# Retention decode: query-times-state products in blocks of eight, and a value-spreading product of 128 rows

## The chip, the core and the metric

The kernel runs on one core of one Trainium2 chip. The metric is the time of one execution on the device, in microseconds (us). A core has TensorE for matrix products (PE in the profile, its weight loads PEld), VectorE (DVE), ScalarE (ACT), GpSimd (POOL) and SyncE (SP), and sixteen DMA engines that move data between HBM and the on-chip memory. The engines run side by side and wait for each other through semaphores; each engine takes its own instructions in the order in which they stand.

## What is computed

One inference step of a two-layer decoder for a new sequence of 256 tokens and for eight decode samples of one token each, 264 columns in all. Layer 0 mixes by RWKV-7, layer 1 by retention; before and after each mixer stands half a SwiGLU. The change touches layer 1's mixer. Its four heads have keys of 256 and values of 512. Cut to the samples, the reference computes for each head and each of the eight samples:

```
q = rotate(x @ wq); k = rotate((x @ wk) / 16); v = x @ wv
S = S * g_head + outer(k, v)          # state [256, 512], read from and written to HBM
o = q @ S                             # [512]
out = (silu(x @ wg) * head_norm(o)) @ wo
```

All is float32. The large products (x @ w) are made of three one-pass products of values split in a high and a low part; the small ones are plain float32 products, each of which stands in the trace as two records.

## The kernel before

**The stream.** All weights pass as 364 units of eight 128x128 tiles through `wt` (L184): SP loads a unit into one of three `raw` buffers, ACT rounds it into `hi` (L89), DVE takes the rest into `lo` (L104), three buffers each, and TensorE makes three products of 264 columns for each tile (`mm3`, L136).

**Who sets the order.** `weave` (L198) writes the program out: a main generator with the large products, and side generators whose steps are put between them when the kernel's own estimate of the engines' times says that they are ready; `mm` (L135) gives the estimate of a product. The framework then orders each engine's instructions once more at compile time by a model of its own. `keep_in_program_order` ties an instruction behind the one that was written before it on its engine, and nothing ties the products.

**Retention.** `retnet` (L1186) makes, head by head, q, k, v and a gate as the main stream (`stream`, L1213). Beside it, `attend` (L1289) makes a head's 256 new tokens, and `decode` (L1366) its eight samples. At the start of a head `attend` turns the samples' rows of v (partitions 0 to 7) into `vr`, a tile of 40 partitions: the high parts at partitions 0 to 7, the low parts at 32 to 39 and zeros between them, which ACT writes anew for each head. For a sample b, `decode` then spreads its row over all 128 partitions with one one-pass product (`pv = sel[:, b, :].T @ vr`, 40 rows, 512 columns), ACT scales the state S (128 x 2 x 512: two halves `kt` of the keys), DVE adds `k * v` to each half (L113), and POOL's queue sends the new state out (L1385). After each pair of samples come four products of q with the states, one for each half of the keys and each sample of the pair: 128 rows, 32 columns of the array, 512 columns of S. Each writes its own quarter of the partitions of one PSUM tile, so a set of four fills the array's four column groups, and the four pairs of a head add up there. `qm` holds the q columns with zeros around them.

**State buffers.** The 32 states pass through ten buffers (`NSB`), loaded by SP in the queue of the weights (`load`, L1168). Six are loaded ahead; the step of sample i asks for state i+6, which takes the buffer of sample i-4 and so waits until that one's products with q, and its transfer out, are done.

Of the kernel before, what the change touches and what calls it, by code (L numbers as in the profile page):

```python
# [40 lines left out]
class Step:  # L41
    def __init__(self, ctx, nc, tc, io):
# [9 lines left out]
        self.late = nc.gpsimd   # the queue of transfers that wait for results  # L52
# [13 lines left out]
    def use(self, m):  # L66
        """the estimates' factors on an engine's times, and the times from an engine to the next"""
        self.model = m
        self.factor = dict(pe=m["PEF"], dve=m["DVEF"], act=m["ACTF"], pool=1.0)
        self.lag = dict(pe=m["LP"], dve=m["LD"], act=m["LA"], pool=0.15)  # L70
# [16 lines left out]
    def act(self, out, in_, func=AF.Copy, scale=1.0, bias=None):  # L87
# [3 lines left out]
        if table != self.table:  # L91
            self.tc.keep_in_program_order(ins)   # no more changes of table than there are in this order
# [30 lines left out]
    def vec(self, name, in_, out, **kw):  # L123
        """another operation of the vector engine"""
        ins = getattr(self.nc.vector, name)(in_=in_, out=out, **kw)
        self.pin(ins)
        self.spent("dve", 0.07 + (0.0064 if name == "reciprocal" else 0.00104) * cols(in_), out, in_)

    def turn(self, out, in_):
        """32x32 blocks transposed"""  # L130
# [4 lines left out]
    def mm(self, out, lhsT, rhs, start=True, stop=True):  # L135
        self.nc.tensor.matmul(out=out, lhsT=lhsT, rhs=rhs, start=start, stop=stop)  # L136
        m, n = cols(lhsT), cols(rhs) / 2400
        if rhs.dtype == F32R:
            us = n + 0.003
        elif m > 64:  # L140
            us = max(4 * n, 0.215)
        else:
            us = max(4 * n * 0.66, 0.09) if m > 32 else 0.035
# [13 lines left out]
    def split(self, raw, first=False):  # L157
        hi = self.hi_p.tile([128, UT, 128], F32R, tag="hi", name="hi")
        lo = self.lo_p.tile([128, UT, 128], F32R, tag="lo", name="lo")
        now, start, self.start = self.now, self.start, 0.0   # it runs ahead  # L160
# [11 lines left out]
    def wt(self, key, k, m, whole=False):  # L172
        """A tile in its two parts, or as it is for a float32 product."""
# [12 lines left out]
    def beside(self, rank, *gs):  # L186
        """more steps for between, those of a lower rank first"""
# [10 lines left out]
    def weave(self, main, sides=()):  # L198
        """Issues main's steps and, between them, the steps of self.sides. A step that yields a key goes on when that
        key is marked; else when its instructions should be through, and the yielded microseconds over."""  # L200
# [56 lines left out]
    def feed(self, f, gain, tail=None):  # L257
        """x[f] has its new value: its square sum, and its parts times the gain; the tail's columns stand behind them."""
# [34 lines left out]
    def setup(self):  # L293
# [8 lines left out]
        # the first weights and inputs, in the order of their use; meanwhile products of nothing keep TensorE's clock up  # L302
# [14 lines left out]
    def preload(self, func):  # L317
        """the table of a function that comes soon"""
        self.act(self.one, self.eps6, func)

# [66 lines left out]
def pack_x(a):  # L387
    """[tokens, 1024] -> [128, 8, tokens]"""
# [35 lines left out]
class Rwkv(Step):  # L424
    def rw_consts(self, p):
        """[128, n] columns by name."""
# [11 lines left out]
    def rwkv(self, gain):  # L438
# [6 lines left out]
        with ExitStack() as ctx:  # L445
# [22 lines left out]
            # 0.5 w0, 0.5 a0, 0.5 ka, 1 - 0.5 ka  # L468
# [9 lines left out]
            # T's tiles: zeros that no product writes  # L478
# [3 lines left out]
            # per pair of heads: [., halves, chunk, 64] operands of the chunks' transitions, with their identities  # L482
# [11 lines left out]
            # lora inputs by linearity: xs @ W = h @ W + (prev - h) @ (mu W)  # L494
# [13 lines left out]
            # of the eight samples, feature-major: log d, kk, -kk a, k', r, v  # L508
# [3 lines left out]
            sto = P1.tile([128, KT, 64], F32, name="sto")   # final states, [key, value]  # L512
# [9 lines left out]
            def stream():  # L522
# [3 lines left out]
                for k0, k1 in ((0, TU["RK"]), (TU["RK"], KT)):  # L526
# [5 lines left out]
                    if rs is None:  # L532
                        rs = self.rms()
                        # normalised inputs, their differences to the step before, and the mixes
# [52 lines left out]
                # the sum, at first without the last heads  # L587
# [90 lines left out]
            # k = xk @ wk, four output tiles at a time, and the lengths of k * k_k per head  # L678
# [26 lines left out]
            # decays and rates of a pair of heads  # L705
# [31 lines left out]
            # alpha, beta, kappa  # L737
            def stage(f):
# [12 lines left out]
                # k' = k (1 - ka + ka a), a = (1 + ta) / 2  # L751
# [15 lines left out]
                # A = alpha beta', token-major: what is below the diagonal, by 32x32 blocks  # L767
# [12 lines left out]
            # T = (I - A)^-1 = I + T A: the 32x32 blocks on its diagonal by substitution, a block on two partitions, one for  # L780
            # the even and one for the odd rows; the rest of each 64x64 by products
            both = lambda t: (t[:, 0:512], t[:, 512:1024])

            def inverse(g):
# [17 lines left out]
                # X[c, i] = T[i, c]  # L802
# [42 lines left out]
            # v token-major, on the other half's partitions  # L845
# [26 lines left out]
            # the state after a chunk and its rows are products of the state before and the chunk's values with one matrix  # L872
            # [keys and earlier steps, (keys, steps)]: first that matrix, then the recurrence
# [4 lines left out]
            def head(f):  # L878
# [12 lines left out]
                # earlier steps' beta' with rho and alone  # L891
# [7 lines left out]
                # alpha kappa' and alpha  # L899
# [8 lines left out]
                # T times both  # L908
# [23 lines left out]
                for c in range(NC):  # L932
                    if c == 2:
                        yield f"L{f}1"
                        # the bonus of a step for itself
# [13 lines left out]
                # group norm per head, token-major  # L949
# [18 lines left out]
                # y = (norm * g + b + bonus) * gate  # L968
# [18 lines left out]
            # one step for the eight samples: 128 rows (half, pair, sample), [value, key] states  # L987
# [8 lines left out]
            def states_with(row, out):  # L996
                """the old states' products with a key each"""
# [26 lines left out]
            def decode_rows():  # L1024
                """S' r = S (d r) + (S kk) (b r) + v (k' r)"""
# [42 lines left out]
    def new_states(self, pool):  # L1068
        """S' = S d + (S kk) b' + v k'"""
# [43 lines left out]
def eye():  # L1113
    """[(j h n), (i c)]: a block's even or odd rows of the identity"""
# [4 lines left out]
def consts():  # L1119
    """Constants of the shapes alone."""  # L1120
# [29 lines left out]
def pack_wkv(s):  # L1150
    """[b, (f e), v, k] -> [(e f b), (v k)]"""
# [10 lines left out]
class Ret(Rwkv):  # L1162
# [21 lines left out]
    def retnet(self, gain):  # L1184
        nc, tc, ps_ = self.nc, self.tc, self.ps
        xg = self.xg  # L1186
        with ExitStack() as ctx:
# [9 lines left out]
            sel = P1.tile([40, NS, 128], F32R, name="sel")  # L1197
            s40 = P1.tile([40, NS], F32, name="s40")
            self.tt(s40, ident[0:40, 0:NS], ident[0:40, 32:32 + NS], ALU.add)
            self.act(sel, s40.unsqueeze(2).to_broadcast([40, NS, 128]))  # L1200
# [12 lines left out]
            def stream():  # L1213
# [36 lines left out]
                # the sum, at first without the last head  # L1250
# [38 lines left out]
            def attend(h, q, k, v):  # L1289
                yield f"v{h}"  # L1290
                # v's sample rows in two parts at partitions 0 and 32
# [3 lines left out]
                vr = P.tile([40, DV], F32R, tag="vr", name="vr", bufs=2)  # L1295
                self.act(vr, c[0:40, RC["dmat"]:RC["dmat"] + DV], scale=0.0)
# [3 lines left out]
                # token-major v  # L1300
# [232 lines left out]
```

## Time and profile before

| | us |
|---|---|
| three runs | 1349.78, 1350.78, 1352.82 |
| median of the runs | 1350.78 |
| the profiled execution: its span from first to last instruction | 1357.0 |
| in it: retention beside the stream | about 870 to 1098 |
| TensorE busy, share of the span | 97% |
| VectorE busy | 66% |
| ScalarE busy | 51% |

The profile is one execution of the program. Of it the trace has the span alone, and nothing of what lies around it; the span stands 6.2 us above the median of the runs. A matrix product's record begins when it starts and ends at a modelled time, and products overlap; so starts are compared with starts below. A row of the timeline with "x2" or more merges records of one kind that follow each other.

### The profile page before, as it was taken

To read this page: it belongs to the slowest core of one execution; us is meant where nothing else is said; L and a number is where in the kernel's file an instruction comes from. 1 tells how busy PE (TensorE), PEld (TensorE's weight loads), DVE (VectorE), ACT (ScalarE), POOL (GpSimd) and SP (SyncE) were. 2 spreads that over 40 slices of the span, in tenths; PEclk is the share of its full clock that TensorE was granted. 3 is DMA by queue.
4 is the path that set the end of the run, shared out by engine and by line. 5 is a ranking of instruction groups with operands and counts; after the bars stand their busy time and mean duration, and the time that the engine had idled before them with its cause. 6 is when DMAs were issued, how large, how long until landed. Compare 5 with 4: busy or idle time off the path is not lost.

```text
span 1357.0 us, 26335 instructions
## 1 busy us (share of the span) xinstructions
PE 1320.5 (97%) x10620; PEld 1210.4 (89%) x10620; DVE 898.0 (66%) x1564; ACT 688.8 (51%) x1239; POOL 95.8 (7%) x205
## 2 busy tenths in 40 slices
PE   8999999998989999999999999999999989999996
PEld 8999998687778999999999999867677679999996
DVE  6666567698776777765666656666676846666654
ACT  6444542633556777744555444536463435544442
POOL 0000002322440000000000000011100100000000
PEclk8999999999987999999999999999999989999998
DMA  6555544334340566665567555676867535555552
GB/s 204 188 178 181 185 157 152 97 110 127 111 112 25 184 216 214 211 201 174 184 220 232 182 177 185 239 258 233 266 240 241 204 123 181 177 185 177 183 181 85
DMA packets 75322, 243.54 MB, mean 179 GB/s; under 512 B 16208, under 2 KB 16464, under 8 KB 75072
## 3 DMA queue, kind: packets, MB, share of 16 engines
q1 hardware_dynamic: 68896, 219.41, 50.9%
q0 software_dynamic: 6128, 21.83, 4.2%
q8 instruction: 83, 1.36, 0.4%
q10 hardware_dynamic: 176, 0.62, 0.1%
q14 instruction: 39, 0.32, 0.1%
HBM read 217.38 MB, written 22.35 MB: 177 GB/s over the span
## 4 chain that ended last, share of the span: by engine, by line
PE 85%; DVE 8%; DMA 3%; ACT 2%; issue 2%; SPq 0%; DVEq 0%; ACTq 0%
PE ps L136 84%; DVE Xd L104 1%; DVE W L104 1%; PE ps L147 1%; DVE lo L104 1%; DMA raw<-in_w 1%; DMA W<-in_eye 1%; DMA rcst<-in_rcst 1%; DMA S<-in_ret 0%; DMA x<-in_x 0%; ACT hi L89 0%; DVE L L104 0%; DMA Sd<-in_wkv 0%; ACT L89 0%; DMA out_swkv<-Sd 0%
## 5 line engine op out<-in xcount | busy, mean ns | idle before, releaser
L89 ACT ACTIVATE hi<-raw 128x1024 fp32r<-128x1024 f32 (+1 forms) x343 | 361.8, 1056 | 477.1 <-PE ps L136 264.6
L104 DVE TENSOR_TENSOR lo<-raw,hi 128x1024 fp32r<-128x1024 f32 (+1 forms) x343 | 421.1, 1228 | 235.2 <-ACT hi L89 233.7
L136 PE MATMUL ps<-ah,hi 128*128 128x264 f32 (+1 forms) x1824 | 530.0, 291 | 3.1 <-ACT ah L89 1.7
L136 PE MATMUL ps<-ah,lo 128*128 128x264 f32 (+1 forms) x1824 | 520.1, 287 | 1.3 <-DVE lo L104 1.3
L136 PE MATMUL ps<-al,hi 128*128 128x264 f32 (+1 forms) x1824 | 519.6, 286 | 0.0
L136 PEld LDWEIGHTS ps<-ah,hi 128*128 128x128 f32 x1824 | 344.9, 189 | 26.2 <-issue 19.0
L136 PEld LDWEIGHTS ps<-al,hi 128*128 128x128 f32 x1824 | 345.3, 189 | 10.1 <-issue 9.7
L136 PEld LDWEIGHTS ps<-ah,lo 128*128 128x128 f32 x1824 | 344.1, 189 | 10.5 <-issue 8.0
L136 PE MATMUL ps<-hh,hi 128*128 128x264 f32 x832 | 238.8, 287 | 0.0
L136 PE MATMUL ps<-hl,hi 128*128 128x264 f32 x832 | 238.7, 287 | 0.0
L136 PE MATMUL ps<-hh,lo 128*128 128x264 f32 x832 | 238.3, 286 | 0.0
L136 PEld LDWEIGHTS ps<-hl,hi 128*128 128x128 f32 x832 | 158.3, 190 | 0.0
L136 PEld LDWEIGHTS ps<-hh,lo 128*128 128x128 f32 x832 | 158.2, 190 | 0.0
L136 PEld LDWEIGHTS ps<-hh,hi 128*128 128x128 f32 x832 | 157.8, 190 | 0.1
L104 DVE TENSOR_TENSOR h<-s,ps 128x264 f32<-128x264 f32 x88 | 37.2, 428 | 47.1 <-PE ps L136 45.7
L113 DVE SCALAR_TENSOR_TENSOR S<-ps,ks,S 128x512 f32<-128x512 f32 x64 | 44.9, 745 | 7.6 <-PE ps L136 7.1
L104 DVE TENSOR_TENSOR t<-ps,rs 128x264 f32<-128x264 f32 x88 | 37.2, 430 | 18.1 <-PE ps L136 18.0
L89 ACT ACTIVATE S<-S 128x1024 f32<-128x1024 f32 x32 | 33.5, 1052 | 16.8 <-DMA S<-in_ret 15.0
L136 PE MATMUL ps<-S,qm 128*32 128x512 f32 x128 | 42.0, 605 | 0.0
L89 ACT ACTIVATE s<-t 128x264 f32<-128x264 f32 x88 | 35.5, 411 | 5.5 <-DVE t L104 5.5
L89 ACT ACTIVATE hh<-h 128x264 fp32r<-128x264 f32 x88 | 35.4, 408 | 4.3 <-DVE h L104 4.3
L104 DVE TENSOR_TENSOR hl<-h,hh 128x264 fp32r<-128x264 f32 x88 | 37.1, 428 | 0.4
(229 smaller groups left out, 1323.8 us busy)
## 6 DMA issues: line engine op xcount, KB each, us to landing
raw<-in_w SPq DMA_DIRECT2D x363, 512.0 KB, 3.7
S<-in_ret SPq DMA_DIRECT2D x32, 512.0 KB, 5.8
out_sret<-S POOLq DMA_DIRECT2D x32, 512.0 KB, 3.4
dS<-in_wkv SPq DMA_DIRECT2D x8, 512.0 KB, 5.6
Sd<-in_wkv SPq DMA_DIRECT2D x4, 512.0 KB, 5.1
out_swkv<-Sd POOLq DMA_DIRECT2D x4, 512.0 KB, 4.1
out_pret<-so POOLq DMA_DIRECT2D x8, 256.0 KB, 3.9
rcst<-in_rcst SPq DMA_DIRECT2D x1, 1100.0 KB, 6.9
```

Of the source, the lines that this page charges most:

```text
L89: ins = self.nc.scalar.activation(out=out, in_=in_, func=func, scale=scale, **kw)
L104: ins = self.nc.vector.tensor_tensor(out=out, in0=a, in1=b, op=op)
L113: ins = self.nc.vector.scalar_tensor_tensor(out=out, in0=a, scalar=s, in1=b, op0=op0, op1=op1)
L136: self.nc.tensor.matmul(out=out, lhsT=lhsT, rhs=rhs, start=start, stop=stop)
L147: self.nc.tensor.transpose(out, in_, ident)
```

## The change

The diff also takes out comments and docstrings through the whole file, which changes nothing; what is left is this.

- `decode` makes the products of q with the states after every four samples (`GROUP = 2` pairs) and no more after every two: eight in a row, two for each column group, latest pair and latest half first. All but the first of the eight are tied behind the one before on TensorE.
- `mm` has a parameter for that tie, and a new estimate for a product of at most 64 columns of the array and 512 columns of data: 0.235 us in place of 0.035.
- `sel` and `vr` have 128 partitions and no more 40. `vr` is two tiles that are zeroed once by POOL, at the start of retention, and are used in turn by the heads; ACT's zeros of each head go.

```diff
-    def mm(self, out, lhsT, rhs, start=True, stop=True):
-        self.nc.tensor.matmul(out=out, lhsT=lhsT, rhs=rhs, start=start, stop=stop)
+    def mm(self, out, lhsT, rhs, start=True, stop=True, behind=False):
+        ins = self.nc.tensor.matmul(out=out, lhsT=lhsT, rhs=rhs, start=start, stop=stop)
+        if behind:
+            self.tc.keep_in_program_order(ins)
...
+        elif n > 0.2:
+            us = 1.1 * n
         else:
             us = max(4 * n * 0.66, 0.09) if m > 32 else 0.035
...
-            sel = P1.tile([40, NS, 128], F32R, name="sel")
-            s40 = P1.tile([40, NS], F32, name="s40")
-            self.tt(s40, ident[0:40, 0:NS], ident[0:40, 32:32 + NS], ALU.add)
-            self.act(sel, s40.unsqueeze(2).to_broadcast([40, NS, 128]))
+            sel = P1.tile([128, NS, 128], F32R, name="sel")
+            s128 = P1.tile([128, NS], F32, name="s128")
+            self.tt(s128, ident[:, 0:NS], ident[:, 32:32 + NS], ALU.add)
+            self.act(sel, s128.unsqueeze(2).to_broadcast([128, NS, 128]))
+            vrs = [P1.tile([128, DV], F32R, name=f"vr{i}") for i in range(2)]
+            for t in vrs:
+                nc.gpsimd.memset(t.bitcast(F32), 0.0)
...
-                vr = P.tile([40, DV], F32R, tag="vr", name="vr", bufs=2)
-                self.act(vr, c[0:40, RC["dmat"]:RC["dmat"] + DV], scale=0.0)
+                vr = vrs[h % 2]
...
-                for j in range(NS // 2):
-                    for b in (2 * j, 2 * j + 1):
+                for j0 in range(0, NS // 2, GROUP):
+                    for b in range(2 * j0, 2 * (j0 + GROUP)):
...
-                    for kt in range(2):
-                        for r in range(2):
-                            g = 64 * kt + 32 * r
-                            self.mm(po[g:g + 32, :], qm[:, kt, 2 * j + r, :], self.state(h, 2 * j + r)[:, kt, :], j == 0, j == NS // 2 - 1)
+                    last = j0 + GROUP - 1
+                    for j in range(last, j0 - 1, -1):
+                        for kt in (1, 0):
+                            for r in (1, 0):
+                                g = 64 * kt + 32 * r
+                                self.mm(po[g:g + 32, :], qm[:, kt, 2 * j + r, :], self.state(h, 2 * j + r)[:, kt, :],
+                                        j0 == 0 and j == last, last == NS // 2 - 1 and j == j0,
+                                        behind=(j, kt, r) != (last, 1, 1))
...
+GROUP = 2
```

## Rows read from the trace of the kernel before

**Rows 1.** The page's first part (busy time, share of the span, instructions of each engine) and its fourth (the chain of work that ended last, by engine).

```profile
PE 1320.5 (97%) x10620; PEld 1210.4 (89%) x10620; DVE 898.0 (66%) x1564; ACT 688.8 (51%) x1239; POOL 95.8 (7%) x205
...
PE 85%; DVE 8%; DMA 3%; ACT 2%; issue 2%; SPq 0%; DVEq 0%; ACTq 0%
```

**Rows 2.** Busy time by stretch: the stretch, its length, busy us and instructions of each engine, TensorE's granted clock as a share of full speed, the DMA engines' busy share, GB/s. The first row is the feed-forward's end and retention's start, the second the whole of retention with its samples, the third the samples of one head.

```profile
840.00:870.00 30.00, 29.56 (x235) 28.73 (x233) 20.82 (x35) 14.03 (x19) 2.89 (x6) 1.00 0.61 207
...
870.00:1097.90 227.90, 225.84 (x1329) 160.32 (x1327) 149.78 (x246) 110.12 (x174) 24.64 (x55) 0.99 0.69 237
...
945.00:980.00 35.00, 35.00 (x206) 23.98 (x203) 24.46 (x41) 15.80 (x29) 3.58 (x8) 1.00 0.88 291
```

**Rows 3.** Groups of instructions by line in the stretch 870 to 1100: line, engine, operation, out<-in, shapes, count, busy us, mean ns of one, idle time before them.

```profile
L113 DVE SCALAR_TENSOR_TENSOR S<-ps,ks,S 128x512 f32<-128x512 f32 x64 | 44.9, 745 | 7.6 <-PE ps L136 7.1
...
L136 PE MATMUL ps<-S,qm 128*32 128x512 f32 x128 | 42.0, 605 | 0.0
...
L136 PE MATMUL ps<-vr,sel 40*128 40x512 f32 x32 | 15.6, 493 | 1.7 <-DVE vr L104 1.7
```

**Rows 4.** TensorE's timeline, head 0: start us, length, operation, count. A query product alone (two records) and a value-spreading product, each between products of the stream.

```profile
899.76 0.28 PE L136 MATMUL ps<-al,hi 128*128 128x264 f32 x1
899.88 0.28 PE L136 MATMUL ps<-ah,lo 128*128 128x264 f32 x1
900.10 1.04 PE L136 MATMUL ps<-S,qm 128*32 128x512 f32 x2
901.07 0.39 PE L136 MATMUL ps<-ah,hi 128*128 128x264 f32 x1
901.30 0.29 PE L136 MATMUL ps<-al,hi 128*128 128x264 f32 x1
901.43 0.28 PE L136 MATMUL ps<-ah,lo 128*128 128x264 f32 x1
901.64 0.50 PE L136 MATMUL ps<-vr,sel 40*128 40x512 f32 x1
902.07 0.39 PE L136 MATMUL ps<-ah,hi 128*128 128x264 f32 x1
902.30 0.28 PE L136 MATMUL ps<-al,hi 128*128 128x264 f32 x1
```

**Rows 5.** The same view: a whole set of four query products (eight records), and the last piece of the last head; between the two, the timeline has 40 such groups of records in all.

```profile
892.02 1.07 PE L136 MATMUL ps<-S,qm 128*32 128x512 f32 x8
893.01 0.39 PE L136 MATMUL ps<-ah,hi 128*128 128x264 f32 x1
...
1093.22 1.05 PE L136 MATMUL ps<-S,qm 128*32 128x512 f32 x2
1094.20 0.39 PE L136 MATMUL ps<-ah,lo 128*128 128x264 f32 x1
```

**Rows 6.** The same view: a value-spreading product with two query products right behind it.

```profile
912.05 0.28 PE L136 MATMUL ps<-ah,lo 128*128 128x264 f32 x1
912.26 0.50 PE L136 MATMUL ps<-vr,sel 40*128 40x512 f32 x1
912.69 1.05 PE L136 MATMUL ps<-S,qm 128*32 128x512 f32 x4
913.67 0.39 PE L136 MATMUL ps<-ah,hi 128*128 128x264 f32 x1
913.90 0.28 PE L136 MATMUL ps<-al,hi 128*128 128x264 f32 x1
```

**Rows 7.** One tile's instructions, with least, median and most ns: the zeros that ACT writes into `vr`, and POOL's zeros of `qm`. Below them the stretch of retention's start, as in rows 2.

```profile
L89 ACT ACTIVATE vr<-rcst x4: 614/631/633, 854.1 to 971.9; 40x512 fp32r<-40x512 f32 x4
...
L1369 POOL MEMSET qm<- x4: 525/526/536, 847.3 to 1041.6; 128x512 f32 x4
...
855.00:860.00 5.00, 4.56 (x35) 4.13 (x35) 4.30 (x6) 4.42 (x6) 0.00 (x0) 1.00 0.07 25
```

**Rows 8.** Who waited for whom in the stretch 850 to 1110: us in total, times, longest. The first three are SP's own queue (L153 is the weights' load, L1172 the states').

```profile
SPq L153 <- DVE lo L104: 126.6, 31, 7.9
SPq L1172 <- PE ps L136: 20.0, 17, 3.1
SPq L1172 <- DMA out_sret<-S: 4.1, 4, 2.6
...
ACT hi L89 <- PE ps L136: 74.6, 28, 6.1
...
ACT hi L89 <- DMA raw<-in_w: 7.6, 3, 3.7
...
PEld ps L136 <- DVE S L113: 2.8, 4, 0.8
```

**Rows 9.** Busy time by stretch as in rows 2: the stretch with the highest DMA rate.

```profile
870.00:875.00 5.00, 5.00 (x44) 4.94 (x43) 1.66 (x2) 2.48 (x4) 0.00 (x0) 1.00 1.00 376
```

**Rows 10.** TensorE's timeline at the end of retention, and the stretch in which it runs slow (as in rows 2).

```profile
1097.61 0.28 PE L136 MATMUL ps<-ah,lo 128*128 128x264 f32 x1
1101.60 0.68 PE L147 MATMUL ps<-rcst,on 64*128 64x64 f32 x4 [3.71 <-DVE on L119]
1102.21 0.59 PE L136 MATMUL ps<-hh,hi 128*128 128x264 f32 x1
1102.60 0.42 PE L136 MATMUL ps<-hl,hi 128*128 128x264 f32 x1
1102.82 0.42 PE L136 MATMUL ps<-hh,lo 128*128 128x264 f32 x1
...
1105.00:1110.00 5.00, 5.00 (x31) 5.00 (x31) 1.59 (x3) 1.06 (x1) 0.00 (x0) 0.68 0.00 0
```

## The prediction

> **What bounds the kernel.** I read the page first: TensorE is busy 97% of the span and holds 85% of the chain that ended last [rows 1]. Then busy time by stretch, to see whether "busy" means the same everywhere. It does not: from 840 to 870 TensorE begins 235 records in 30 us and its weight loads fill 28.73 us of them; in retention TensorE is busy 225.84 of 227.90 us, but with 1329 records, and the loads fill 160.32 [rows 2]. Nothing else is full there: VectorE 149.78, ScalarE 110.12 us, the DMA engines 0.69 of their time. So TensorE sets retention's pace, yet something holds it that is not the stream's work. By line, two small groups stand out, 128 records of query products and 32 value-spreading ones [rows 3]. The timeline shows what they cost: the reader is to compare starts.
>
> **A query product today.** In the stream a product starts 0.12 us after the one before (899.76, 899.88). Around one query product the starts are 899.88, 900.10, 901.07, 901.30 [rows 4]: from the stream's product before to the second one behind it 1.42 us, where two steps of the stream take 0.24. So this piece costs 1.18 us: 0.97 until the stream goes on, and 0.10 and 0.11 at its two edges. A whole set of four (eight records) takes 0.99 in place of 0.97 [rows 5]: four products in four column groups run side by side, and one alone costs as much as four. Now the count: 16 sets should be 16 pieces, but the timeline has 40 [rows 5]. In each head the first set stands together and each of the three later ones falls into pieces of one, two and one product, with the stream or transposes between; the compile-time order starts each product when its half of a state is ready. Today: 40 x 1.18 = 47.2 us.
>
> **The blocks of eight.** The first product of a block waits for the last half of the last state; when it can go, the seven others can, and they are tied behind it. So I expect 2 blocks in each of 4 heads. No block of eight is in this trace. From above: two rounds of a set, 2 x 0.99, and one pair of edges, 0.21: 2.19 us; with the edges paid twice, 2 x 1.18 = 2.36. From below: if eight ran like four, 0.99 + 0.21 = 1.20. Each column group has two products to do one behind the other, so I take 2.19: 8 x 2.19 = 17.5 us (9.6 to 18.9). **Gain 29.7 us** (28.3 to 37.6).
>
> **The value-spreading product.** Starts 901.43, 901.64, 902.07, 902.30 [rows 4]: 0.87 us from product to second product, less 0.24, is 0.63; 32 of them are 20.2 us. It is a one-pass product like the stream's, with 512 columns where those have 264: by columns it should cost 0.12 x 512/264 = 0.23. What the two kinds differ in besides is 40 rows against 128. If the stops at its edges come from the rows, 128 rows end them: 32 x 0.23 = 7.4, a gain of 12.8; if not, nothing is gained. I take 0.23, since the product nearest to the new one is the stream's, with the same 128 rows and array columns. In five places it stands beside a query piece and shares an edge: starts 912.05 to 913.90 give 1.61 in place of 1.18 + 0.63 = 1.81 [rows 6], so some 0.2 are counted twice there, and twice more in a place with three: about 2 us off both. **Gain 10.8 us** (-2 to 12.8).
>
> The Trainium skill speaks against this half: in "TensorE: Matmul & The Clock Gate", section "Why this matters for your kernels", a single product of few rows takes the time of one with 128, and only running several together gains. By that the sum below would lose its 10.8 us. The Trainium skill's "TensorEngine Tiling (Array Packing)", section "Tiling Modes", says that a change of tiling mode drains the engine; by that the sum would keep them. The 0.21 before and the 0.43 and 0.23 behind the 40-row product [rows 4] side with the second.
>
> **What costs nothing.** ACT's zeros go: 4 x 0.63 us [rows 7]. Two of them stand in the start of retention, where TensorE misses 0.44 us of 5 [rows 7]; at most that is won, I take none. POOL's two memsets, 0.53 us each by the row of `qm` [rows 7], lie where POOL has nothing else; if they were late, the first head's spreading would wait up to 1.1 us. `sel` is made by the same one instruction of ACT on as many columns. The new estimate in `mm` moves side steps among the stream's products; it adds no work.
>
> **What the saved time meets.** Sum on TensorE: 29.7 + 10.8 = 40.5 us off 227.9, leaving 187. VectorE's 149.8 would be 80% of that, and 54 MB (237 GB/s x 227.9 us) would need 289 GB/s, where 376 were moved for 5 us [rows 2, 9]. The weights have reserve: SP waits 126.6 us for buffers and ACT 74.6 for TensorE to free `hi`, ACT for a weight's landing only 7.6 [rows 8]. Locally it is tighter: from 945 to 980 VectorE is busy 24.46 of 35 us [rows 2], and these 35 hold six samples and nine pieces: 9 x 1.18 + 6 x 0.40 less one and a half new blocks is 9.7 us that go there, which leaves 24.5 in 25. A state update that is late then holds a block, and with it all that is queued on TensorE behind it; today such waits are 2.8 us in all [rows 8]. One update of two halves is 2 x 0.745 = 1.5 us [rows 3]; if each of eight blocks waited one, 12 us. I take a third, **4 us lost** (0 to 12).
>
> At the end of retention TensorE idles 3.7 us for the last head's norm, and then runs at half clock (2.4 to 1.2 GHz): the starts 1102.60 and 1102.82 are 0.22 apart, until about 1108 [rows 10]; some 25 products lose 0.1 each. These 6 us hang on how much of the stream stands behind the last block; I count 0, between a gain of 6 and a loss of 4.
>
> **Sum.** 40.5 - 4 = 36.5 us off the profiled span of 1357.0: 1320.5. The trace shows nothing around the span, and the span stands 6.2 us above the median of the runs; I carry the difference over: 1350.8 - 36.5 = 1314.
>
> **Rivals.**
> 1. VectorE becomes the bound in the samples' stretches. For it: 24.5 in 25 us; against it: 20% of reserve over the whole, and a stream that can run ahead. If each block waits 2.5 us (an update and a weight's `lo` ahead of it), 20 us are lost: gain 20, 1330.
> 2. The 128-row product keeps its edges: gain 29.7 - 4 = 26, 1325. For it: no product of its shape is in the trace; against it: the stream's one-pass products have no such edges.
> 3. Slower: the states' loads stop the weights. After sample 4 state 10 is asked for, whose buffer is free only after the block that ends with sample 3; until now it waited for a pair that was done two samples earlier, some 10 us. The load stands in SP's queue, and all weight loads behind it. Today these waits are 20.0 us in 17, at most 3.1 [rows 8]. TensorE has three split units before it, 3 x 24 x 0.12 = 8.6 us; from a wait beyond that it idles. At 14 us each, 8 times 5.4 us are lost, and 2.5 more at half clock each time, 63 in all: 1350.8 - 40.5 + 63 = 1373. It decides the sign from 5.1 us of loss for each block, a wait of 11.2 us. Against it: the block stands in TensorE's order before sample 4's spreading.
> 4. The blocks don't hold together: the ties give an order, not a bar to others between. In four pieces each they cost 8 x 4 x 1.18 = 37.8, the gain shrinks by 20: 1334.
>
> **How the numbers follow.** The forecast, 1304 to 1322, has 0.62; rival 1 0.16; rival 2 0.08; rival 3 0.05; rival 4 0.06; and 0.03 that more is won, down to 1297 (blocks at the low end, and the idle end gone). The low end 1303 is a gain of 40.5 + 6 with nothing lost; the high end 1332 takes in rivals 1 and 2. Faster or slower means by over 0.2% (2.7 us), about what a measurement of this kernel can tell from no change. Slower is rival 3, 0.05; no change is rival 4 with some six pieces in each block (8 x 6 x 1.18 = 56.6, which takes 39 back), half of its chance, 0.03; all else is faster, 0.92.
>
> **What would show it.** Eight groups of 16 records of query products, the stream's next product 1.9 to 2.1 us after each starts; the spreading product 0.12 behind the stream and the next 0.23 behind it; TensorE's record count in the head's stretch per us up by a fifth; weight loads filling more of retention. Wrong would be: groups of fewer records, waits of TensorE on the state update above 12 us, SP's waits at L1172 above 8 us each, or idle TensorE with the clock at half behind it.

## The result, and the profile after

The changed kernel takes 1305.72 us (median of four runs, 1304.99 to 1306.51); the kernel before, on the same chip, 1350.94 (four runs, 1349.78 to 1352.82). The ratio is 0.9665, with a 95% interval of 0.9652 to 0.9677: 45.2 us less, where 36.5 were forecast (1314, range 1303 to 1332). The profiled execution took 1305.14 us, of which its span is 1303.3.

The page of the kernel after: its first part (busy time, share of the span, instructions) and, from its fourth, the chain by engine. They answer to [rows 1].

```profile
PE 1271.8 (98%) x10620; PEld 1199.1 (92%) x10620; DVE 895.9 (69%) x1564; ACT 690.7 (53%) x1237; POOL 99.1 (8%) x207
...
PE 88%; DVE 6%; DMA 2%; issue 1%; ACT 1%; SPq 0%; DVEq 0%; ACTq 0%
```

TensorE begins the same 10620 records and is busy 48.7 us less. It did not get less work; it got rid of time in which a record stood over it and nothing new began. Busy time by stretch of the kernel after shows where, with the columns of [rows 2]: the feed-forward's end, retention with its samples, the samples of one head, and the stretch with the highest DMA rate.

```profile
840.00:870.00 30.00, 30.00 (x249) 29.84 (x248) 21.89 (x35) 15.05 (x18) 4.72 (x8) 1.00 0.72 245
...
865.00:1056.00 191.00, 188.59 (x1373) 159.10 (x1371) 150.91 (x252) 113.92 (x175) 25.34 (x55) 1.00 0.79 287
...
930.00:955.00 25.00, 25.00 (x203) 21.66 (x202) 22.11 (x37) 13.78 (x21) 3.75 (x10) 1.00 0.95 345
...
905.00:910.00 5.00, 5.00 (x42) 3.33 (x40) 2.47 (x5) 3.50 (x6) 1.77 (x5) 1.00 1.03 417
```

In retention 1373 records begin in 191.0 us, 7.2 per us, where it was 1329 in 227.9, 5.8 per us [rows 2]; the weight loads fill 83% of it and no more 70%. In the samples of a head VectorE is now busy 22.11 of 25 us, which is tight, and TensorE still has no idle time there.

TensorE's timeline of the kernel after shows the two new pieces: a block of sixteen records, and a value-spreading product, each between products of the stream. They answer to [rows 4, 5].

```profile
949.87 0.28 PE L137 MATMUL ps<-ah,lo 128*128 128x264 f32 x1
950.09 1.92 PE L137 MATMUL ps<-S,qm 128*32 128x512 f32 x16
951.94 0.39 PE L137 MATMUL ps<-ah,hi 128*128 128x264 f32 x1
952.17 0.28 PE L137 MATMUL ps<-al,hi 128*128 128x264 f32 x1
...
980.58 0.28 PE L137 MATMUL ps<-ah,lo 128*128 128x264 f32 x1
980.70 0.40 PE L137 MATMUL ps<-vr,sel 128*128 128x512 f32 x1
980.94 0.28 PE L137 MATMUL ps<-ah,hi 128*128 128x264 f32 x1
981.06 0.28 PE L137 MATMUL ps<-al,hi 128*128 128x264 f32 x1
```

Read by starts, as ahead of the prediction: from 949.87 to 952.17 are 2.30 us, less two steps of the stream (0.24) 2.06: a whole block, at the price of less than two of the old pieces. The spreading product starts 0.12 behind the stream and the stream goes on 0.24 behind it; its edges are gone, and it costs 0.12 + 0.24 + 0.12 - 0.24 = 0.24 (0.23 in most places). There are eight such blocks, all whole.

Who waited for whom in the stretch 830 to 1070 of the kernel after (us in total, times, longest), as in [rows 8]. L158 is the weights' load, L1177 the states'.

```profile
SPq L158 <- DVE lo L104: 96.7, 28, 7.3
...
SPq L1177 <- DMA out_sret<-S: 6.4, 5, 1.9
...
SPq L1177 <- PE ps L137: 5.0, 10, 1.4
...
ACT hi L89 <- PE ps L137: 46.5, 28, 3.4
...
PE ps L137 <- ACT oT L89: 2.0, 1, 2.0
...
PE ps L152 <- DVE on L119: 0.4, 1, 0.4
```

No row has TensorE waiting for a state update (`DVE S`); 2.0 us in one place are a wait for ScalarE. SP waits 5.0 us for TensorE to free states, where it was 20.0. The weights' reserve has shrunk (ACT's wait for a free `hi` is 46.5, was 74.6) and is not used up.

The end of retention in the kernel after, in TensorE's timeline, answers to [rows 10]:

```profile
1055.39 0.28 PE L137 MATMUL ps<-hh,lo 128*128 128x264 f32 x1
1055.60 0.46 PE L152 MATMUL ps<-rcst,on 64*128 64x64 f32 x4
1055.99 0.39 PE L137 MATMUL ps<-hh,hi 128*128 128x264 f32 x1
1056.22 0.28 PE L137 MATMUL ps<-hl,hi 128*128 128x264 f32 x1
1056.34 0.28 PE L137 MATMUL ps<-hh,lo 128*128 128x264 f32 x1
```

The idle 3.71 us ahead of the last head's transposes are gone, and the clock stays whole: the steps behind are 0.12, not 0.22. Between the last block and these transposes now stand 36 products of the output sum; before, none did.

**Two measures for what follows.** The *stage* is the distance between the starts of VectorE's reciprocals of the token norms before and behind retention, from one profiled execution. For the kernel after they are:

```profile
850.75 1.80 DVE L125 RECIPROCAL rs<-sd 128x264 f32<-128x264 f32 x1
...
1113.06 1.80 DVE L125 RECIPROCAL rs<-sd 128x264 f32<-128x264 f32 x1 [0.56 <-ACT sd L89]
```

that is 262.3; before, 855.66 and 1165.73, 310.1. Of the 53.7 us between the two spans 47.8 lie in this stage, 1 behind it and 5 ahead of it, where the change does nothing: the profiled execution of the kernel before was a long one. With the 1.8 us that the kernel after has around its span it took about 1358.8 us, 7.9 above the median. Inside the stage, too, something is its own: behind the 1.7 us wait for `vr` [rows 3] its clock was at half until 883 (22 records from 879 to 884, mean granted clock 0.66), which no other profiled execution has at that place; 11 steps of 0.22 there alone lost 1.1 us. And the stage has a blur of up to 3 us, because its marks are VectorE's: at the first of them TensorE had begun 7212 records in the kernel before, 7197 in the kernel after, and 7189 to 7213 in the fourteen executions, with 0.12 us from one to the next. The *cost of the pieces* is the start-to-start price of each query or spreading piece as above, summed over all, with waits ahead of a piece in it: 68.3 before, 26.5 after.

### The profile page after: what moved, and what is told of

Same layout as the page of the kernel before. It is cut to its first block, busy times and chain, and to the rows that moved or that the text cites. A ratio compares the mean times of both kernels' runs of the same rounds, so it can differ in the third digit from the quotient of the medians.

```text
span 1303.3 us, 26335 instructions
## 1 busy us (share of the span) xinstructions
PE 1271.8 (98%) x10620; PEld 1199.1 (92%) x10620; DVE 895.9 (69%) x1564; ACT 690.7 (53%) x1237; POOL 99.1 (8%) x207
## 4 chain that ended last, share of the span: by engine, by line
PE 88%; DVE 6%; DMA 2%; issue 1%; ACT 1%; SPq 0%; DVEq 0%; ACTq 0%
PE ps L137 87%; DVE Xd L104 1%; DVE W L104 1%; PE ps L152 1%; DMA W<-in_eye 1%; DVE L L104 1%; DMA x<-in_x 0%; DMA Sd<-in_wkv 0%; DVE lo L104 0%; DMA raw<-in_w 0%; ACT hi L89 0%; DMA out_swkv<-Sd 0%; DMA st<-ka 0%; DVE nm L113 0%; DVE Ab L131 0%
## 5 line engine op out<-in xcount | busy, mean ns | idle before, releaser
L104 DVE TENSOR_TENSOR h<-s,ps 128x264 f32<-128x264 f32 x88 | 37.2, 428 | 47.0 <-PE ps L137 45.8
L137 PE MATMUL ps<-xv,raw 128*128 128x264 f32 x128 | 34.1, 411 | 0.0
```

The costliest lines, as they stand in the source:

```text
L104: ins = self.nc.vector.tensor_tensor(out=out, in0=a, in1=b, op=op)
L137: ins = self.nc.tensor.matmul(out=out, lhsT=lhsT, rhs=rhs, start=start, stop=stop)
```

## The experiments

The theory at first was the prediction's: the ties hold each block together, 128 rows end the edges of the spreading product, and the two gains add. The first rival: not the ties but the order in which the eight are written holds them, latest half first. The second: the gain beyond the forecast comes from the end of retention, which was counted at nothing. Times are medians; "before" is the kernel before, run beside it on the same chip, and a difference is one of medians. The ratio takes in all executions, and where their spread is uneven it gives another difference: 13.1 us for experiment 1, 33.0 for 2, 45.8 for 4 and 7.6 for 10.

**1. The spreading product alone.** The kernel before with `sel` and `vr` of 128 partitions and without ACT's zeros; its query products are untouched.

```diff
-            sel = P1.tile([40, NS, 128], F32R, name="sel")
+            sel = P1.tile([128, NS, 128], F32R, name="sel")
...
-                vr = P.tile([40, DV], F32R, tag="vr", name="vr", bufs=2)
-                self.act(vr, c[0:40, RC["dmat"]:RC["dmat"] + DV], scale=0.0)
+                vr = vrs[h % 2]
```

> The kernel before with one part of the change: sel and vr on 128 partitions, vr zeroed once by POOL; pairs of samples, estimate and order of the query products as before. Theory (the stops at the edges of the value-spreading product come from its 40 rows): the product costs 0.22 us in place of 0.62, 32 x 0.40 = 12.8, about 1338 us; the query products stay in 40 pieces of 1.18. Rival (the stops come with any product of 512 columns between those of 264, and the whole gain comes from the blocks): edges stay, 1351 us.

Measured: 1336.05 us (1334.36 to 1338.16) against 1350.44, ratio 0.9903 [0.9877, 0.9929]: -14.4. The stage is 15.3 shorter, the pieces 13.0 cheaper (68.3 to 55.3, 1.7 of it the wait for `vr` in [rows 3], which is gone too); all 40 query pieces are still there. The 128 rows alone take away the edges.

**2. The blocks alone.** The kernel after with the 40-row `sel` and `vr` and ACT's zeros back.

```diff
-            sel = P1.tile([128, NS, 128], F32R, name="sel")
+            sel = P1.tile([40, NS, 128], F32R, name="sel")
...
-                vr = vrs[h % 2]
+                vr = P.tile([40, DV], F32R, tag="vr", name="vr", bufs=2)
+                self.act(vr, c[0:40, RC["dmat"]:RC["dmat"] + DV], scale=0.0)
```

> The changed kernel with sel and vr of 40 partitions and ACT's zeros as before; blocks of eight, ties and estimate kept. Theory (cost goes by pieces): 8 groups of 16 records, 40 x 1.18 - 8 x 2.05 = 30.8 us less than before and some 5 us more from the end of retention, where TensorE no longer idles: 1315 to 1320 us. Rival (the two halves of the change need each other, for instance because a 40-row product inside a stretch breaks a block): less than 25 us, above 1326.

Measured: 1316.34 (1313.95 to 1318.94) against 1350.44, ratio 0.9756 [0.9729, 0.9784]: -34.1. Eight whole blocks, spreading products at 0.62, pieces 29.4 cheaper, and no idle time at the end. The stage is 35.9 shorter, 6.5 more than its pieces: the first sign that the end carries some 6 us. The two parts together would be -48.5 by the medians and -46.1 by the ratios, and the whole change is -45.2: they add to within 1 to 3 us.

**3. Tied sets of four.** The kernel after with a block for each pair.

```diff
-GROUP = 2
+GROUP = 1
```

> The changed kernel with GROUP = 1: a set of four after every two samples, tied, latest half first. Theory A (what matters is that a set stands whole, and a block of eight saves only one pair of edges for each two sets): 16 groups of 8 records at 1.19 = 19.0 in place of 8 x 2.05 = 16.4, 2.6 us slower than the changed kernel, about 1308. Theory B (the eight in a row are what brings the gain, as the name of the change says): half of the blocks' 30 us is lost, 1318 or more.

Measured: 1312.65 (1309.93 to 1314.76) against 1350.44, ratio 0.972 [0.9694, 0.9747]. There are 16 whole groups of eight records at 1.19 us, and the pieces cost 27.5, one us more than in the kernel after; but the time is 6.9 us above that kernel's. TensorE's timeline of this kernel says where it is, and busy time by stretch what it drew behind it:

```profile
1053.63 0.28 PE L137 MATMUL ps<-ah,lo 128*128 128x264 f32 x1
1057.62 0.69 PE L152 MATMUL ps<-rcst,on 64*128 64x64 f32 x4 [3.71 <-DVE on L119]
```

```profile
1060.00:1065.00 5.00, 5.00 (x27) 5.00 (x27) 1.60 (x6) 1.54 (x3) 0.00 (x0) 0.58 0.00 0
```

The idle end is back, the same 3.71 us as before, with the clock at 0.58 of full speed behind it. So whole sets of four already bring the fall in pieces, but the time of neither theory came out: what is left hangs on the end of the stage. (The 0.58 is the mean of a stretch that has both levels of the clock; where it is at half, steps are 0.22 us.)

**4. No ties.** The kernel after, written in the same order, with nothing tied.

```diff
-                                        behind=(j, kt, r) != (last, 1, 1))
+                                        behind=False)
```

> The changed kernel without the ties behind the first product of a block; all else kept, the order in which the eight are written too. Theory A (only the ties hold a block together): the compile-time order starts each product when its state is ready, some four to six pieces for each block; 8 x 5 x 1.18 = 47 in place of 16.4, about 1336 us. Theory B (the order of writing, latest last half first, or the number of samples is enough): 8 groups of 16 records still, 1306 us.

Measured: 1303.43 (1301.88 to 1305.26) against 1350.44, ratio 0.9661 [0.9635, 0.9687]; the whole change has 0.9665. Again eight groups of sixteen, and by tile and shape all 10620 records of TensorE stand in the order of the kernel after. The theory that the ties hold the blocks fell; with this order of writing they do nothing that can be measured. Whether they would hold blocks that are written in the old order was not tried.

**5. Only the order, in the kernel before.** The four products of a pair are written latest half first; nothing else is changed.

```diff
-                    for kt in range(2):
-                        for r in range(2):
+                    for kt in (1, 0):
+                        for r in (1, 0):
```

> The kernel before with one thing changed: the four query products of a pair are written latest half and latest sample first. No ties, no new estimate, four and not eight, 40 rows. The run without ties kept whole blocks, so something else holds them. Theory A (the order of writing: the first product needs the half that DVE writes last, and when it can go all others can): 16 groups of 8 records, 40 - 16 = 24 pieces of 1.18 less, 28 us: about 1322 us. Theory B (the estimate of the query products' time or the number of eight does it): 40 pieces, 1350 us.

Measured: 1325.5 (1323.82 to 1327.15) against 1351.23, ratio 0.9807 [0.979, 0.9824]: -25.7, from two edited lines. TensorE's timeline of this kernel, two sets:

```profile
896.60 1.07 PE L136 MATMUL ps<-S,qm 128*32 128x512 f32 x8
897.60 0.39 PE L136 MATMUL ps<-ah,lo 128*128 128x264 f32 x1
...
912.12 1.06 PE L136 MATMUL ps<-S,qm 128*32 128x512 f32 x8
913.12 0.39 PE L136 MATMUL ps<-ah,hi 128*128 128x264 f32 x1
```

All 16 sets stand whole, where it was one in each head [rows 5]; the pieces cost 39.7 instead of 68.3 (-28.6), and the stage is 28.4 shorter. So the order of writing decides.

How it does so fits one reading. The four products stand on TensorE in their written order. Written in the old order they need the first half of the pair's first sample, the first half of its second, then the two second halves, while VectorE finishes both halves of one sample before the next. A compile-time order that starts each product when its half is ready in its model then gets pieces of one, two and one product, which is what stands in the three later sets of each head. Written latest first, the other three are ready when the first goes. The split stands in the program and is not made by waits on the chip: in the kernel before, VectorE was done with the second set of head 0 at 898.96 (both halves of sample 3), and its pieces start at 900.10 [rows 4], 902.62 and 904.29:

```profile
897.56 1.40 DVE L113 SCALAR_TENSOR_TENSOR S<-ps,ks,S 128x512 f32<-128x512 f32 x2
...
902.62 1.05 PE L136 MATMUL ps<-S,qm 128*32 128x512 f32 x4
...
904.29 1.05 PE L136 MATMUL ps<-S,qm 128*32 128x512 f32 x2
```

Why the first set of each head stood whole even in the old order is not shown.

**6. Eight, earliest first.** The kernel after with the old order of writing and no ties.

```diff
-                    for j in range(last, j0 - 1, -1):
-                        for kt in (1, 0):
-                            for r in (1, 0):
+                    for j in range(j0, j0 + GROUP):
+                        for kt in range(2):
+                            for r in range(2):
...
-                                        behind=(j, kt, r) != (last, 1, 1))
+                                        behind=False)
```

> The changed kernel without ties and with the eight products written in the old order, earliest pair, first half and first sample first. Theory A (the order of writing holds a block together): pieces again, at least three for each of the 8 blocks, 24 or more. Theory B: 8 groups of 16 records as in the changed kernel.

Measured: 1318.94, one run. TensorE's timeline of this kernel shows how its first block falls apart, into ten, four and two records:

```profile
886.55 1.91 PE L137 MATMUL ps<-S,qm 128*32 128x512 f32 x10
...
888.83 1.05 PE L137 MATMUL ps<-S,qm 128*32 128x512 f32 x4
...
890.60 1.05 PE L137 MATMUL ps<-S,qm 128*32 128x512 f32 x2
```

25 groups instead of eight, pieces 43.1 instead of 26.5. Eight in a row do not hold by their number; with 5, this shows the order to be the cause. Seven of the eight blocks end in a piece of two products and one of one, as the last pair does by the reading under 5.

**7 and 8. How many rows.** The kernel after with `sel` and `vr` of 64 and of 96 partitions.

```diff
-            sel = P1.tile([128, NS, 128], F32R, name="sel")
+            sel = P1.tile([64, NS, 128], F32R, name="sel")
...
-            vrs = [P1.tile([128, DV], F32R, name=f"vr{i}") for i in range(2)]
+            vrs = [P1.tile([64, DV], F32R, name=f"vr{i}") for i in range(2)]
```

> The changed kernel with sel and vr on 64 partitions in place of 128; blocks, ties and estimate kept. Theory A (up to 64 rows the array is used in another shape, which stops TensorE at both edges): the spreading product costs 0.62 us as with 40 rows, 12 us more than the changed kernel, about 1316. Theory B (the cost falls with the rows that lie empty): between, 0.45 or so.

> The changed kernel with sel and vr on 96 partitions. Theory A (from 65 rows on the array is used whole): 0.22 us each as with 128 rows, time as the changed kernel. Theory B (only all 128 rows avoid the edges): 0.62.

Measured, one run each: 1313.44 with 64 rows, 1310.68 with 96. TensorE's timeline, first the kernel with 64 rows, then the one with 96:

```profile
893.83 0.28 PE L137 MATMUL ps<-ah,lo 128*128 128x264 f32 x1
894.05 0.50 PE L137 MATMUL ps<-vr,sel 64*128 64x512 f32 x1
894.48 0.39 PE L137 MATMUL ps<-ah,hi 128*128 128x264 f32 x1
894.70 0.28 PE L137 MATMUL ps<-al,hi 128*128 128x264 f32 x1
```

```profile
898.88 0.28 PE L137 MATMUL ps<-ah,lo 128*128 128x264 f32 x1
899.00 0.40 PE L137 MATMUL ps<-vr,sel 96*128 96x512 f32 x1
899.24 0.29 PE L137 MATMUL ps<-ah,hi 128*128 128x264 f32 x1
899.37 0.28 PE L137 MATMUL ps<-al,hi 128*128 128x264 f32 x1
```

64 rows have the edges of 40 (0.22 before, 0.43 and 0.22 behind: 0.63), 96 those of 128 (0.12, 0.24 and 0.13: 0.25). It is a step between 64 and 96 rows and no slope; 128 rows cost no more than 96. The time of the 96-row run hides this, since its stage started late, at 853.6; the stages are 274.0 with 64 rows and 265.0 with 96.

**9 and 10. The end alone.** The last head's transposes are put off by 5 us of the kernel's own estimate, once in the tied sets of four (experiment 3) and once in the kernel before, where it is the only edit.

```diff
-                yield 0.2
+                yield 5.0 if h + 1 == RH else 0.2
```

> Whole sets of four, tied (GROUP = 1), with one line changed: the last head's step that transposes its samples' normed rows is put 5 us later in the kernel's own plan, so that 36 output products stand before these transposes on TensorE, as they do in the changed kernel. Theory A (blocks of eight bring 2.6 us by themselves, and the other 4 to 5 us between pairs tied and the changed kernel are the idle 3.7 us and the half clock behind it at the end of retention, which depend on what stands before the transposes): no idle stretch there, 6 to 7 us less than pairs tied, 1306 us. Theory B (sets of four lose 7 us in themselves): 1312.

> The kernel before with that one line alone: the last head's transposes stand behind 36 output products. Theory A (the end of retention was worth 3.7 us of idle time and 3.4 us of half clock): 5 to 7 us less than before, 1345. Theory B (the wait only moves, to the output products of the last head that need the same rows): 1350.

Measured against 1351.71: the sets of four take 1306.77 (1304.75 to 1308.7), ratio 0.9668 [0.9651, 0.9684], 5.9 us less than without the edit; the kernel before takes 1342.62 (1341.1 to 1348.68), ratio 0.9944 [0.9927, 0.9961], -9.1. The stages shrink by 7.5 and 8.4. Busy time by stretch behind the transposes, first the sets of four with the late transposes (beside the row of experiment 3), then the kernel before with them (beside the last row of [rows 10]):

```profile
1060.00:1065.00 5.00, 5.00 (x43) 5.00 (x43) 4.08 (x7) 3.14 (x6) 0.00 (x0) 1.00 0.47 170
```

```profile
1095.00:1100.00 5.00, 5.00 (x44) 5.00 (x43) 3.74 (x6) 3.02 (x7) 0.00 (x0) 1.00 0.46 139
```

43 records in 5 us at the full clock in place of 27 at 0.58, and 44 in place of 31 at 0.68. The idle time costs 3.7 us, and the half clock behind it some 3 more: 25 steps lose 0.1 each in experiment 3 and in the kernel before, and the transposes ahead of them a little. The rest of the 7.5 and 8.4 is not the end's: the sets of four also lose a wait of 0.7 us elsewhere, and the kernel before its half clock behind the wait for `vr`. Nor is the half clock of one length: in experiment 1, behind the same 3.71 us, 15 steps ran at half. And the sets of four now reach the kernel after within 1.1 us (stage 263.9 against 262.3), which the times alone can't tell from nothing. Eight blocks cost 16.5 us where 16 sets cost 19.0, but the wait for `oT` (experiment 11) takes back 2.0 of it, where the sets of four wait 0.3.

**11. A later PSUM tile.** In the kernel after, the one wait of TensorE in the samples is 2.04 us for ScalarE's copy of `oT`. The tile of the query products is taken just before a head's first block.

```diff
-                po = ps_()
+                po = None
...
+                    po = ps_() if po is None else po
```

> The changed kernel with the PSUM tile of the query products taken just before a head's first block and not at the head's start; TensorE's order is the same. Theory A (the seventh block's 2.0 us wait on ACT's oT is for the bank that the tile gets, which ACT still reads): the wait goes, 2 us less than the changed kernel, 1303.5. Theory B (ACT is late in any case, and the wait moves to the next product): 1305.5.

Measured: 1302.71 (1301.27 to 1303.39) against 1351.71, ratio 0.9639 [0.9625, 0.9653]. TensorE's timeline of this kernel:

```profile
1031.24 3.09 PE L137 MATMUL ps<-S,qm 128*32 128x512 f32 x16 [2.04 <-ACT oT L89]
```

The wait is still there, and at the same block, so neither theory came out as written. The stage is 264.6, not shorter than after's 262.3, so the time isn't evidence of a gain. The block behind the wait takes 3.09 us here and 1.92 in the kernel after, because here the clock is at half (mean granted clock 0.66 from 1031 to 1036). In the kernel after ScalarE has no idle time from 1032.20 until its copy ends at 1034.47, so the copy may simply be late; what would end the wait stays open.

**12. Sixteen in a row.** The kernel after with all products of a head in one block.

```diff
-GROUP = 2
+GROUP = 4
```

> The changed kernel with GROUP = 4: one block of sixteen for each head. Theory A (only edges count): 4 groups of 32 records at 1.00 + 3 x 0.86 + 0.20 = 3.8, 15.1 us in place of 16.4, about 1304.5; the states' loads wait longer, but not with the weights behind them. Theory B (rival 3 of the prediction): the loads of the states 10 to 13 of each head's second half can go only when the whole head is done, SP's waits at their line reach 10 us, and TensorE idles for weights or states: 1312 or more.

Measured: 1308.48 (1305.81 to 1310.98) against 1351.71, ratio 0.9683 [0.9665, 0.9701]. The pieces cost least of all, 24.6, and the time is still not below the kernel after. TensorE's waits in the stretch 850 to 1070, and the first of them with the half clock behind it:

```profile
PE ps L152 <- DVE on L119: 5.6, 4, 3.7
PE ps L137 <- DVE S L113: 1.2, 1, 1.2
```

```profile
927.34 1.27 PE L152 MATMUL ps<-rcst,on 64*128 64x64 f32 x6 [3.75 <-DVE on L119]
928.27 0.77 PE L137 MATMUL ps<-vr,sel 128*128 128x512 f32 x1
928.84 0.42 PE L137 MATMUL ps<-ah,hi 128*128 128x264 f32 x1
929.06 0.42 PE L137 MATMUL ps<-al,hi 128*128 128x264 f32 x1
```

What the longer block saves in pieces goes to idle time at a head's transposes, as at the old end, with steps of 0.22 behind it. SP waits for TensorE to free states 5.1 us in nine, at most 1.4: even a block twice as long does not stop the weights.

**The telling ones beside each other** (us; time against before on the same chip, and stage and pieces of one execution each):

| | time | stage | pieces | idle at the end |
|---|---|---|---|---|
| before | 0 | 310.1 | 68.3 | 3.7 |
| sel_alone | -14.4 | 294.7 | 55.3 | 3.7 |
| pairs_reversed | -25.7 | 281.7 | 39.7 | 3.7 |
| pairs_tied | -37.8 | 271.4 | 27.5 | 3.7 |
| blocks_alone | -34.1 | 274.2 | 38.9 | none |
| before_late | -9.1 | 301.7 | 67.6 | none |
| pairs_late | -44.9 | 263.9 | 27.5 | none |
| after | -45.2 | 262.3 | 26.5 | none |
| no_ties | -47.0 | 264.8 | 28.0 | none |

Where the idle end stands, the stage falls by what the pieces save, to within 2.3 us (28.4 against 28.6 in pairs_reversed); where it is gone, by 5.0 to 7.7 us more.

## Why the prediction was right, and where it was not

**The blocks of eight: right in number and size, wrong in their reason.** 40 pieces became eight, at 2.06 us where 2.19 was taken, 16.5 us in all for the forecast's 17.5; the low end, eight at the price of four (1.20), is excluded. The step that failed is the sentence "when it can go, the seven others can, and they are tied behind it": its first half holds and is the whole cause (experiments 4, 5 and 6), its second half does nothing here. Taken seriously, the first half alone would have told that the old sets of four fell apart by their order of writing, and that two lines bring back 25.7 us of the 45.

**The spreading product: right.** 0.23 to 0.24 as forecast. In experiment 1 the pieces fell by 13.0 us, and by 11.3 without the wait for `vr`; 10.8 was forecast. That this wait went with the change was counted at nothing; but a row of the waits has it again, at 1.0 to 1.2 us, in the runs of experiments 8 and 11, which have no ACT zeros either, so it does not hang on these alone. Against the page "TensorE: Matmul & The Clock Gate" of the Trainium skill, section "Why this matters for your kernels", a single product of few rows did not take the time of one with 128: 0.63 to 0.23. The Trainium skill's "TensorEngine Tiling (Array Packing)", section "Tiling Modes", lists a mode for 64 rows, and says that a change of mode drains the engine; experiments 7 and 8 agree, with the step between 64 and 96 rows. That it is this drain, and no other stop at the same border, is not shown.

**"A third, 4 us lost": mis-sized, it was 0.** No wait of TensorE for a state update is left, where 4 us were taken off for late ones. The 2.04 us for `oT` is another wait, and in size it takes the place of the 1.7 us for `vr` in [rows 3]. VectorE was rightly seen as tight: 22.11 of 25 us, where 24.5 were worked out. The tenth that is left was enough, and rival 1 did not come.

**The end "I count 0, between a gain of 6 and a loss of 4": mis-sized, it is a gain of some 6 us.** The rows for it were all there [rows 10]: 3.7 us idle, 25 products at half clock. That it would go was not foreseen; experiments 9 and 10 show its price by itself. In the kernel after, the stage is 47.8 shorter and its pieces save 41.8, for which 40.5 were forecast. 6.0 remain, about the price of the end; nearer than the blur of the stage that is not shown.

**Was it luck?** Not in its size: the two large terms, 40.5 forecast and 41.8 measured, make up nearly all of the 45.2 us. The two small terms were wrong by 4 and 6 us on the same side and did not hide each other; they are why the kernel after lies near the low end of the range. The reason given for whole blocks was wrong in its half on the ties, and that cost the forecast nothing, since the change also reverses the order of writing, which holds them.

**The rivals.** The edges went (2 fell), the blocks are whole (4 fell). The slower one, that the states' loads stop the weights, has nothing for it: SP's waits for TensorE to free states fell from 20.0 us to 5.0, the longest 1.4, where it decides from 11.2 for each block. The reason named against it holds: the block stands in TensorE's order before the next sample's spreading, so the state's buffer is free when SP comes to it.

**What the clock did in single executions.** The stage is 2.5 us longer without the ties (264.8), though the time is not and TensorE's records stand in the same order. 1.5 of these us lie in its pieces (28.0 against 26.5): behind the same 2.04 us wait for `oT` the clock fell to half there, and the block took 3.14 us where the kernel after has 1.92 (from 1034.57). Busy time by stretch in that kernel:

```profile
1030.00:1035.00 5.00, 5.00 (x27) 2.37 (x28) 3.12 (x6) 1.11 (x3) 0.54 (x1) 0.66 0.62 213
```

The runs of experiment 8 with 96 rows and of experiment 11 have the same half clock behind this wait; the kernel after, with 1.00 from 1035 to 1040, has not. The other 1.0 us is the blur of the stage: at its start TensorE stood eight records further back without the ties (7189 against 7197). So the same wait, with the same records behind it, costs its own length in one execution and 1.5 us more in another.

**What stays open.** What ends the wait for `oT`; why a block of eight puts the last head's transposes behind the 36 output products; what the new estimate in `mm` does by itself, which no run takes out alone (experiment 5 has whole sets without it); and a few us of spread between chips and executions, which is more than the kernels after, no_ties, pairs_late and po_late differ by.

## What to carry to other kernels

If a scheduler may put other work between accumulating products, write first the one whose operand is ready last; that alone kept sets of four together, while tying them as well, or adding more to a block, brought little. A small product between products of the full array pays for its edges; try it with more rows (filled with zeros) if its neighbours have 128: here 96 and 128 rows had no edges, 40 and 64 had. And when pieces are taken out of a stage, look at what then stands ahead of the last dependent chain at its end: an idle of 3.7 us cost some 3 us more in a halved clock.

## What the runs showed of the hardware that was not expected

- Four products side by side in the array's column groups cost 1.19 us from stream to stream, eight 2.06, sixteen 3.8: some 0.9 for each four more, and 0.3 once. One alone costs 1.18, as much as four.
- The DMA engines of this one core moved 417 GB/s for five microseconds (905 to 910 in the kernel after), where the kernel before had 376 in its busiest five [rows 9].
- The start of the stage, ahead of which all these programs do the same work, lies between 845.2 and 855.7 us in fourteen executions, with stretches at half clock of different number and length ahead of it. So one profiled span tells less of a change than its stage does.
- A wait of 2.04 us was followed by half clock in three profiled executions (no_ties, po_late and 96 rows) and not in a fourth (the kernel after). In the kernel before a wait of 1.7 us was followed by it; waits of 1.8 us (blocks_alone and 64 rows) were not.
